# First down-projection weights split ahead of the last up chunk's convolution, kept sums added to the residual while weights stream, six pairs in the closing products

## The chip, the cores and the metric

The kernel runs on one core of one Trainium2 chip. The metric is the device time of one execution, in microseconds (us); lower is better. The time before is 957.09 us, the median of three runs between 956.24 and 958.12. Engines are named as in the profile: PE (matrix products), DVE (vector), ACT (scalar), POOL (GpSimd), SP (issues most transfers), and PSUM is the memory of eight banks into which PE sums.

## What is computed

A one-layer encoder trunk on 512 tokens of width 1024. The change lies in its last part, the gated MLP with a causal convolution, and in the residual and layer norm behind it:

```
z = h @ w_up                                  # 512 x 1024 by 1024 x 5632
zc = conv_b + sum_k conv_w[k] * shifted(z)    # three taps along the sequence
val, gate = split(zc)                         # 2816 each
y = (silu(gate) * val) @ w_down               # 2816 x 1024
x = layer_norm(ALPHA * x + gt_f * y) * ln_f_g + ln_f_b
```

Each product of 32-bit numbers is made from halves: an operand is cast to a short "hi" part (on ACT), the rest is its "lo" part (a subtraction on DVE), and three products hi·hi, hi·lo, lo·hi are summed.

## The kernel before, in words

**Up-projection.** The 44 column chunks of `w_up`, m = 0 to 43, are taken two by two, a value chunk and a gate chunk. Each takes 24 matmuls (`pzu`, L115, L116, L118). Its convolution follows: ACT takes the first tap out of PSUM (`zc`, L1521), DVE adds the other two (L1524, L1528). Then ACT does the silu (L1542), POOL multiplies gate and value (L1543). Two such products make one of eleven "pairs", p = 0 to 10, whose combinations are split into hi and lo: `xa` comes from the first product alone, `yh`, `xs`, `xh`, `ys` and their lo parts (L1458 to L1482) wait for the second one.

**Down-projection.** It is a product of 2 x 2 blocks done with seven products instead of eight (m1 to m7). The first sweep runs over the pairs and sums m1, m5, m6, m7, for two row tiles each, in all eight PSUM banks (`pd`). A step of it (`sweep_step`, L1583 on) is 24 matmuls and needs the pair's weights, which come by SP (`db0`, `db1`, `da`), are cast on ACT (`dbh`, `dah`) and subtracted on DVE (`dbl`, `dal`; L1559, L1560). Behind steps, `ahead` fetches and splits what the second sweep will need: the weights of pairs that are kept (`dr`, split into `d2..`, `d3..`, `d4..`, L1576, L1577) and, by POOL's transfers, left operands that had been written out (`z`, L1614). Step p = 10 ends the sums; `evacuate` takes them out of PSUM as `u1`, `u4`, `u3` and `c22` (L1667 to L1677).

The second sweep sums m2, m3, m4 (`pe`): for six pairs the weights (`dc`, `dd`) are streamed and split the same way, 18 matmuls a pair; for the R2 = 5 kept pairs the products are left to the end, where `close` makes them row tile by row tile. For each tile and half `final` then adds `u` to the bank (DVE, L1728), multiplies by the gate row `gt_f` (POOL, in the last row DVE, L1729), adds it to ALPHA·x (`residual`, DVE, L1688) and takes statistics (L1693); `row_end` (L1736 to L1757) does the layer norm and sends a row of tiles out. Three halves need no product of the second sweep's end and are done earlier, while pairs stream: `whole_half` for the two `c22` (POOL L1696, DVE L1688) and one `u3` (POOL L1723).

A scheduler sorts the instructions of each engine by the dependences and by priorities; each engine then does its list in order, and PE, ACT, DVE, POOL and SP wait for each other by semaphores. SP issues its transfers in its own list's order, so an issue that waits holds those behind it.

Of the kernel before, what the change touches and what calls it, by code (L numbers as in the profile page):

```python
# [15 lines left out]
P = 128  # L16
# [35 lines left out]
def trunk(ctx: ExitStack, tc: tile.TileContext, A, out):  # L52
# [22 lines left out]
    def pt_t(name, dt=F32):  # L75
        return sb.tile([P, 512], dt, name=name, tag="pt", bufs=8)
# [4 lines left out]
    def f(ap):  # L81
        return ap.bitcast(F32)
# [29 lines left out]
    def mm_chunk(o, wh, wl, xh, xl):  # L112
        cs = [slice(k * P, (k + 1) * P) for k in range(KT)]
        for k, c in enumerate(cs):
            nc.tensor.matmul(o, wh[:, c], xl[k], start=k == 0, stop=False)  # L115
            nc.tensor.matmul(o, wh[:, c], xh[k], start=False, stop=False)  # L116
        for k, c in enumerate(cs):
            nc.tensor.matmul(o, wl[:, c], xh[k], start=False, stop=k == KT - 1)  # L118
# [1372 lines left out]
    def ada_wide_piece(idx, k):  # L1491
# [3 lines left out]
        for n in range(2):  # L1495
# [4 lines left out]
            else:  # L1500
# [2 lines left out]
                    op0=ALU.mult, op1=ALU.add,  # L1503
                )

    held = [None]
    for i in range(NP):
        half = []
        for v in range(2):
            m = 2 * i + v  # L1510
            if m < NE:
                if v == 0:
                    up_early((m, m + 1), 1)
                pz = pzs[m]
# [6 lines left out]
            nc.scalar.activation(  # L1521
                t, pz, AF.Identity, bias=cols[:, cc + 3 : cc + 4], scale=cols[:, cc + 2 : cc + 3]
            )
            nc.vector.scalar_tensor_tensor(  # L1524
                out=t[:, 1:512], in0=pz[:, 0:511], scalar=cols[:, cc + 1 : cc + 2],
                in1=t[:, 1:512], op0=ALU.mult, op1=ALU.add,
            )
# [12 lines left out]
        if i == 5 + KT + 1:  # L1540
            gate_rows(3, "gtf")
        nc.scalar.activation(gate, gate, AF.Silu)  # L1542
        nc.gpsimd.tensor_tensor(out=val, in0=val, in1=gate, op=ALU.mult)  # L1543
# [8 lines left out]
    R2 = 5
    lo_half, hi_half = slice(0, 512), slice(512, 1024)

    def split_wide(parts, n, name):
        hi = wp.tile([P, D], F32R, name=name + "h", tag="whi")
        lo = wp.tile([P, D], F32R, name=name + "l", tag="wlo")
        for raw, c in parts:
            nc.scalar.copy(out=hi[:, c], in_=raw)  # L1559
            nc.vector.tensor_tensor(out=lo[:, c], in0=raw, in1=f(hi[:, c]), op=ALU.subtract)  # L1560
        return hi, lo

    def whole(src, name):
        raw = wp.tile([P, D], F32, name=name, tag="raw", bufs=3)
        nc.sync.dma_start(out=raw, in_=src)
        return raw

    def block(src, name, alloc=pad_t):
        raw = alloc(name)
        nc.sync.dma_start(out=raw[:, :512], in_=src)  # L1570
        return raw[:, :512]

    def split_block(raw, name, alloc):
        hi = alloc(name + "h")
        lo = alloc(name + "l")
        nc.scalar.copy(out=hi, in_=raw)  # L1576
        nc.vector.tensor_tensor(out=lo, in0=raw, in1=f(hi), op=ALU.subtract)  # L1577
        return hi, lo

    def wdn_row(k, c):  # L1580
        return A["wdn"][k * P : (k + 1) * P, c]
# [29 lines left out]
    def reload(p):  # L1611
        left2[p] = [act_t(f"z{i}{p}") for i in range(3)]
        for dst, src in zip(left2[p], spill[p]):
            nc.gpsimd.dma_start(out=dst, in_=src)  # L1614

    ws2 = {}

    def second_weights(p, alloc):
        srcs = ((2, wdn_row(2 * p + 1, lo_half)), (3, wdn_row(2 * p + 1, hi_half)), (4, t4_t[p]))
        raws = [(c, block(src, f"dr{c}", pt_t)) for c, src in srcs]  # L1620
        ws2[p] = {c: split_block(raw, f"d{c}{p}", alloc) for c, raw in raws}

    ahead = [(second_weights, HP - R2, h_t)]
    for i in range(R2 - 1):
        ahead += [(second_weights, HP - R2 + 1 + i, act_t), (reload, i)]
    ahead.append((reload, R2 - 1))
    free = 1 + 6
    for p in range(HP - 1):
        rb = [block(wdn_row(2 * p, lo_half), "db0"), block(t3_t[p], "db1")]
        ra = whole(wide_t[p], "da")  # L1630
        wb_ = split_wide(zip(rb, (lo_half, hi_half)), D, "db")
        wa_ = split_wide(((ra, slice(0, D)),), D, "da")
        x = lefts1(p)
        sweep_step(p, (
            (wb_, ((m1, x[1], lo_half), (m7, x[7], hi_half))),
            (wa_, ((m6, x[6], lo_half), (m5, x[5], hi_half))),
        ))
        while ahead and free >= (need := 6 if ahead[0][0] is second_weights else 3):
            work, *args = ahead.pop(0)
            work(*args)  # L1640
            free -= need
        free += 4
    p = HP - 1
    rb = [block(wdn_row(2 * p, lo_half), "db0"), block(t3_t[p], "db1")]
# [47 lines left out]
    def statistics(t, slot, n, c=slice(0, 512)):  # L1692
        return nc.vector.bn_stats(out=stats[t][:, slot, :], in_=x1[t][n][:, c])  # L1693

    def whole_half(t):
        nc.gpsimd.tensor_tensor(out=c22[t], in0=c22[t], in1=gt_f[1], op=ALU.mult)  # L1696
        residual(2 + t, 1, c22[t])
        if t == 0:
            statistics(2, 0, 1)
        else:  # L1700
            for i in range(2):
                statistics(3, i, 1, slice(i * 256, (i + 1) * 256))

    m2, m3, m4 = ([ps(f"pe{c}") for _ in range(2)] for c in (2, 3, 4))
    for p in range(HP - R2):
        rc = whole(A["wdn"][(2 * p + 1) * P : (2 * p + 2) * P, :], "dc")
        rd = block(t4_t[p], "dd")
        wc_ = split_wide(((rc, slice(0, D)),), D, "dc")
        wd_ = split_wide(((rd, lo_half),), 512, "dd")
        x = lefts2(p)  # L1710
        sweep_step(p, (
            (wc_, ((m2, x[2], lo_half), (m3, x[3], hi_half))),
            (wd_, ((m4, x[4], lo_half),)),
        ))
        if R2 + p < SPILLED:
            reload(R2 + p)
        if p < 2:
            whole_half(p)
        if p == 2:
            lnfg = row_tiles(4, h_t, "lnfg")  # L1720
            lnfb = row_tiles(5, h_t, "lnfb")
            q = pt_t("fq")
            nc.gpsimd.tensor_tensor(out=q, in0=u3[1], in1=gt_f[0], op=ALU.mult)  # L1723
            residual(3, 0, q)

    def final(t, n, acc, u, op, slot, eng):
        q = pt_t("fq")
        nc.vector.tensor_tensor(out=q, in0=u, in1=acc, op=op)  # L1728
        eng.tensor_tensor(out=q, in0=q, in1=gt_f[n], op=ALU.mult)  # L1729
        residual(t, n, q)  # L1730
        statistics(t, slot, n)

    def row_end(t, count):
# [168 lines left out]
```

## Time and profile before

| what | us |
|---|---|
| median of three runs | 957.09 (956.24 to 958.12) |
| the profiled execution, whole | 957.47 |
| its span in the profile | 955.7 |
| PE busy | 926.9 (97% of the span) |
| DVE busy | 676.0 (71%) |
| ACT busy | 408.6 (43%) |
| POOL busy | 279.2 (29%) |

The whole time holds 1.8 us that lie outside the span. A row of the timeline is: start, duration, engine, line, operation, the tile written and what it is made from, shapes, and in brackets how long the engine had stood idle before it and who released it. A row with "x2" stands for two in a row. A row of windows gives, for a stretch of time, each engine's busy us with its count of instructions, the clock granted to PE (1.00 is full), the busy share of the transfer engines and their GB/s. Lines are those of the kernel before.

### The profile page before, as it was taken

The page shows a single profiled execution, that of the slowest core. Times are in us where ns is not written, and L with a number is a line of the kernel's source. Part 1 is how long each engine was busy: PE and PEld are TensorE (multiplying, and loading weights), DVE is VectorE, ACT ScalarE, POOL GpSimd, SP SyncE. Part 2 cuts the span into 40 slices and gives each one's busy share as a digit, 9 for nine tenths or more (in the row PEclk, how much of TensorE's full clock was granted, in tenths as well). Part 3 has the DMA queues.
Part 4 walks back from the last instruction along what each step waited for, and adds up shares of the span by engine and source line. Part 5 has one row for each costly group of instructions (what it writes and reads, how often), then busy time and mean ns, then how long its engine had stood idle before and what let it go on. Part 6 is the DMA issues. An engine that isn't in the chain of part 4 may idle for free.

```text
span 955.7 us, 12643 instructions
## 1 busy us (share of the span) xinstructions
PE 926.9 (97%) x4453; PEld 780.4 (82%) x4453; DVE 676.0 (71%) x1043; ACT 408.6 (43%) x689; POOL 279.2 (29%) x339
## 2 busy tenths in 40 slices
PE   7999999999999999999999999999999999799993
PEld 6988888888888888888888889988888888588783
DVE  6967668546677798776475688688887566656848
ACT  4576555543324322233323435654444555456311
POOL 3741221122341154402153712122123211111514
PEclk9999999999999999999999999999999999799997
DMA  8913112134447986774575451155554534398902
GB/s 300 344 56 116 49 44 83 38 136 151 138 144 267 344 340 231 248 235 146 163 277 187 154 155 44 46 192 172 175 178 130 159 121 141 121 331 289 371 35 88
DMA packets 68159, 165.78 MB, mean 173 GB/s; under 512 B 9216, under 2 KB 12736, under 8 KB 68096
## 3 DMA queue, kind: packets, MB, share of 16 engines
q1 hardware_dynamic: 56880, 137.54, 42.7%
q0 software_dynamic: 10784, 26.89, 8.0%
q8 instruction: 35, 0.57, 0.2%
q10 hardware_dynamic: 432, 0.55, 0.2%
q14 instruction: 28, 0.23, 0.1%
HBM read 144.16 MB, written 20.78 MB: 173 GB/s over the span
## 4 chain that ended last, share of the span: by engine, by line
PE 82%; DVE 7%; DMA 6%; POOL 2%; issue 1%; ACT 1%; SPq 0%; DVEq 0%; POOLq 0%; ACTq 0%
PE pzu L116 7%; PE pzu L118 7%; PE pzu L115 7%; PE pg L115 4%; PE pg L116 4%; PE pg L118 4%; PE py L118 4%; PE py L115 4%; PE py L116 4%; PE pd L1590 2%; PE pd L1592 2%; PE pd L1593 2%; DMA ada<-in_ada1p 2%; PE pa L115 2%; PE pu L115 2%; PE pu L116 2%
## 5 line engine op out<-in xcount | busy, mean ns | idle before, releaser
L95 DVE TENSOR_TENSOR wupl<-wup,wuph 128x1024 fp32r<-128x1024 f32 x38 | 52.4, 1379 | 24.2 <-PE pzu L118 15.9
L1543 POOL TENSOR_TENSOR zc<-zc 128x512 f32<-128x512 f32 x22 | 29.8, 1354 | 131.4 <-ACT zc L1542 107.5
L94 ACT CAST wuph<-wup 128x1024 fp32r<-128x1024 f32 x38 | 40.1, 1054 | 46.4 <-PE pzu L116 33.9
L94 ACT CAST wbh<-wb 128x1024 fp32r<-128x1024 f32 x24 | 25.3, 1054 | 71.5 <-PE py L116 52.8
L985 POOL DMA_DIRECT2D wt<-wb x44 | 24.5, 556 | 77.1 <-DVE wb L981 72.0
L1521 ACT ACTIVATE zc<-pzu,cols 128x512 f32<-128x512 f32 x44 | 34.0, 777 | 24.9 <-PE pzu L118 20.5
L95 DVE TENSOR_TENSOR wgl<-wg,wgh 128x1024 fp32r<-128x1024 f32 x22 | 29.9, 1358 | 20.8 <-PE pg L118 10.1
L981 DVE TENSOR_TENSOR wb<-wb,wb 128x512 f32<-128x512 f32 x44 | 35.3, 806 | 6.2 <-DMA wb<-in_wdn 5.7
L1524 DVE SCALAR_TENSOR_TENSOR zc<-pzu,cols,zc 128x511 f32<-128x511 f32 x44 | 32.5, 743 | 9.3 <-ACT zc L1521 9.1
L856 DVE SCALAR_TENSOR_TENSOR ada<-adar,cact,ada 128x512 f32<-128x512 f32 x42 | 38.7, 961 | 0.4 <-DMA adar<-in_ada 0.4
L95 DVE TENSOR_TENSOR wbl<-wb,wbh 128x1024 fp32r<-128x1024 f32 x24 | 31.0, 1292 | 10.7 <-PE pg L118 5.4
L94 ACT CAST wgh<-wg 128x1024 fp32r<-128x1024 f32 x22 | 23.3, 1059 | 32.7 <-PE pg L116 20.3
L775 POOL TENSOR_SCALAR pe<-pe,mx 128x128 f32<-128x128 f32 (+3 forms) x32 | 17.0, 534 | 69.3 <-DVE mx L774 52.4
L1528 DVE SCALAR_TENSOR_TENSOR zc<-pzu,cols,zc 128x510 f32<-128x510 f32 x44 | 32.6, 744 | 0.7
L419 POOL TENSOR_TENSOR mg<-mg,th 128x512 f32<-128x512 f32 x16 | 28.5, 1779 | 12.7 <-DVE th L416 12.5
L1614 POOL DMA_DIRECT2D z<-ys x27 | 14.6, 542 | 56.7 <-PE pd L1590 35.0
L937 POOL TENSOR_TENSOR asum<-apad 128x527 f32<-128x527 f32 x8 | 12.3, 1544 | 54.6 <-ACT apad L932 28.0
L298 DVE SCALAR_TENSOR_TENSOR acc<-ada,cact,acc 128x256 f32<-128x256 f32 (+1 forms) x29 | 27.4, 944 | 1.0
L1542 ACT ACTIVATE zc<-zc 128x512 f32<-128x512 f32 x22 | 13.9, 631 | 23.7 <-DVE zc L1528 23.7
L1160 POOL TENSOR_TENSOR oraw<-oraw,gtt 128x512 f32<-128x512 f32 x6 | 9.8, 1645 | 42.0 <-DMA oraw<-in_wo 42.0
L1182 POOL TENSOR_TENSOR o<-o,gtt 128x512 f32<-128x512 f32 x10 | 17.5, 1772 | 12.2 <-DMA o<-in_wo 12.2
L771 ACT ACTIVATE pe<-sc,mx 128x128 f32<-128x128 f32 (+3 forms) x32 | 16.8, 528 | 8.8 <-DVE mx L769 7.5
(1541 smaller groups left out, 3239.1 us busy)
## 6 DMA issues: line engine op xcount, KB each, us to landing
wup<-in_wup SPq DMA_DIRECT2D x44, 512.0 KB, 3.6
wb<-in_wb SPq DMA_DIRECT2D x24, 512.0 KB, 3.8
adar<-in_ada SPq DMA_DIRECT2D x48, 256.0 KB, 4.8
wg<-in_wg SPq DMA_DIRECT2D x22, 512.0 KB, 3.6
wb<-in_wdn SPq DMA_DIRECT2D x44, 256.0 KB, 4.8
wt<-wb POOLq DMA_DIRECT2D x44, 256.0 KB, 4.0
z<-ys POOLq DMA_DIRECT2D x27, 256.0 KB, 6.8
ada<-in_ada1p SPq DMA_DIRECT2D x24, 256.0 KB, 5.0
```

What stands on the lines that cost most here:

```text
L94: nc.scalar.copy(out=hi[:, :n], in_=raw[:, :n])
L95: ins = nc.vector.tensor_tensor(out=lo[:, :n], in0=raw[:, :n], in1=f(hi[:, :n]), op=ALU.subtract)
L115: nc.tensor.matmul(o, wh[:, c], xl[k], start=k == 0, stop=False)
L116: nc.tensor.matmul(o, wh[:, c], xh[k], start=False, stop=False)
L118: nc.tensor.matmul(o, wl[:, c], xh[k], start=False, stop=k == KT - 1)
L419: nc.gpsimd.tensor_tensor(out=merged[m], in0=merged[m], in1=th, op=ALU.add)
L856: nc.vector.scalar_tensor_tensor(out=acc[n], in0=src, scalar=cact[:, k : k + 1], in1=acc[n], op0=ALU.mult, op1=ALU.add,)
L981: ins = nc.vector.tensor_tensor(out=dst, in0=x, in1=y, op=op)
L1521: nc.scalar.activation(t, pz, AF.Identity, bias=cols[:, cc + 3 : cc + 4], scale=cols[:, cc + 2 : cc + 3])
L1524: nc.vector.scalar_tensor_tensor(out=t[:, 1:512], in0=pz[:, 0:511], scalar=cols[:, cc + 1 : cc + 2], in1=t[:, 1:512], op0=ALU.mult, op1=AL ...
L1528: nc.vector.scalar_tensor_tensor(out=t[:, 2:512], in0=pz[:, 0:510], scalar=cols[:, cc : cc + 1], in1=t[:, 2:512], op0=ALU.mult, op1=ALU.add,)
L1543: nc.gpsimd.tensor_tensor(out=val, in0=val, in1=gate, op=ALU.mult)
```

## The change

It does four things. One: `first_weights(0)` is called after the matmuls of the last up chunk (m = 43) and before its convolution, so that the splits of pair 0's weights stand ahead of that convolution on ACT and DVE; for this the helpers move up in the file. Two: `ahead` takes nothing behind step 0 and at most two items behind each later step. Three: R2 goes from 5 to 6: five pairs stream, six are in the closes (in the order 6, 7, 9, 10, 8, 5), and pair 5's second weights (`d25`, `d35`, `d45`) are fetched at the end of the streamed pairs. Four: `fold` multiplies all eight evacuated sums by the gate row on POOL and adds them to the residual on DVE during streamed pairs 0 to 3, instead of three; `final` then multiplies the bank by the gate on DVE and adds it, with no POOL operation and no `u`.

```diff
+    R2 = 6
...
+    def first_weights(p):
+        rb = [block(wdn_row(2 * p, lo_half), "db0"), block(t3_t[p], "db1")]
+        ra = whole(wide_t[p], "da")
+        wb_ = split_wide(zip(rb, (lo_half, hi_half)), D, "db")
+        wa_ = split_wide(((ra, slice(0, D)),), D, "da")
+        return wb_, wa_
...
                 mm_chunk(pz, uh, ul, h2_hi, h2_lo)
+            if m == 2 * NP - 1:
+                opening = first_weights(0)
             cc = C_CONV + 4 * m
...
-        while ahead and free >= (need := 6 if ahead[0][0] is second_weights else 3):
-            work, *args = ahead.pop(0)
-            work(*args)
-            free -= need
+        for _ in range(2 if p else 0):
+            need = 6 if ahead and ahead[0][0] is second_weights else 3
+            if ahead and free >= need:
+                work, *args = ahead.pop(0)
+                work(*args)
+                free -= need
...
+    def fold(t, n, u):
+        nc.gpsimd.tensor_tensor(out=u, in0=u, in1=gt_f[n], op=ALU.mult)
+        residual(t, n, u)
...
-        if p < 2:
-            whole_half(p)
+        if p == 0:
+            fold_whole(0)
+            fold_whole(1)
+        if p == 1:
+            fold(0, 0, u1[0])
+            fold(1, 0, u1[1])
         if p == 2:
+            fold(0, 1, u4[0])
+            fold(1, 1, u4[1])
...
+        if p == 3:
+            fold(2, 0, u3[0])
+            fold(3, 0, u3[1])
+    second_weights(HP - R2, h_t, pad_t)
+    closing = [HP - 5, HP - 4, HP - 2, HP - 1, HP - 3, HP - 6]
...
-    def final(t, n, acc, u, op, slot, eng):
+    def final(t, n, acc, op, slot):
         q = pt_t("fq")
-        nc.vector.tensor_tensor(out=q, in0=u, in1=acc, op=op)
-        eng.tensor_tensor(out=q, in0=q, in1=gt_f[n], op=ALU.mult)
-        residual(t, n, q)
+        nc.vector.tensor_tensor(out=q, in0=acc, in1=gt_f[n], op=ALU.mult)
+        nc.vector.tensor_tensor(out=x1[t][n], in0=x1[t][n], in1=q, op=op)
         statistics(t, slot, n)
```

Three places show what the lists of the engines make of it. The first is DVE where the up-projection ends; `zc` rows are the convolutions of the last two chunks, and `db`/`da` the weights of pair 0 (before: db_7689 and db_7691; after: db_7655 and db_7657) and pair 1 (after: db_7729). Before:

```order
L1524 SCALAR_TENSOR_TENSOR zc<-pzu,cols,zc 128x511
L1528 SCALAR_TENSOR_TENSOR zc<-pzu,cols,zc 128x510
L1475 TENSOR_TENSOR se<-zc 128x256
L1475 TENSOR_TENSOR sd<-zc 128x256
L1475 TENSOR_TENSOR sd<-se,zc 128x256
L1482 TENSOR_TENSOR yl_7671<-zc,yh_7670 128x512
L1459 TENSOR_TENSOR xs_7667<-se,xs_7667 128x256
L1475 TENSOR_TENSOR se<-zc,sd 128x256
L1480 TENSOR_TENSOR xl_7669<-sd,xh_7668 128x512
L1560 TENSOR_TENSOR dbl<-db_7689,dbh 128x512
L1560 TENSOR_TENSOR dal<-da,dah 128x1024
L1459 TENSOR_TENSOR ys_7672<-se,ys_7672 128x256
```

And after:

```order
L1514 TENSOR_TENSOR dbl<-db_7655,dbh 128x512
L1514 TENSOR_TENSOR dbl<-db_7657,dbh 128x512
L1459 TENSOR_TENSOR xa_7586<-zc,xa_7586 128x256
L1564 SCALAR_TENSOR_TENSOR zc<-pzu,cols,zc 128x511
L1568 SCALAR_TENSOR_TENSOR zc<-pzu,cols,zc 128x510
L1514 TENSOR_TENSOR dal<-da,dah 128x1024
L1564 SCALAR_TENSOR_TENSOR zc<-pzu,cols,zc 128x511
L1568 SCALAR_TENSOR_TENSOR zc<-pzu,cols,zc 128x510
```

Pair 0's subtractions moved ahead of the last convolutions, `dal` directly in front of the last one; where they stood, pair 1's now stand (from db_7729 on). On ACT the casts moved in the same way. The second place is SP's list there; `wt_2216` to `wt_2219` are the `da` weights of pairs 0 to 3, `dr` the weights kept for the second sweep. Before:

```order
L1565 DMA da<-wt_2216 128x1024
L1565 DMA da<-wt_2217 128x1024
L1565 DMA da<-wt_2218 128x1024
L1570 DMA db_7689<-in_wdn 128x512
L1570 DMA db_7691<-wt_2227 128x512
L1570 DMA db_7747<-in_wdn 128x512
L1570 DMA dr_7729<-in_wdn 128x512
```

And after:

```order
L1519 DMA da<-wt_2216 128x1024
L1524 DMA db_7655<-in_wdn 128x512
L1524 DMA db_7657<-wt_2227 128x512
L1519 DMA da<-wt_2217 128x1024
L1519 DMA da<-wt_2218 128x1024
L1519 DMA da<-wt_2219 128x1024
L1524 DMA db_7729<-in_wdn 128x512
L1524 DMA db_7731<-wt_2228 128x512
L1524 DMA db_7787<-in_wdn 128x512
L1524 DMA dr_7769<-in_wdn 128x512
```

Pair 0's `db` moved to the front, and pair 3's `da`, which goes into one of three buffers and so needs pair 0's to be free, now stands ahead of pair 1's two `db`. The third place is POOL behind the first sweep; `z` are the reloads of the second sweep's left operands, `gtf` the gate row. Before:

```order
L1614 DMA z_8353<-ys_5772 128x512
L1614 DMA z_8354<-ys_5773 128x512
L1723 TENSOR_TENSOR fq<-u_8263,gtf_7073 128x512
L1696 TENSOR_TENSOR c_8268<-c_8268,gtf_7075 128x512
L1696 TENSOR_TENSOR c_8274<-c_8274,gtf_7075 128x512
L1614 DMA z_8392<-ys_5774 128x512
```

And after:

```order
L1704 TENSOR_TENSOR u_8238<-u_8238,gtf_7073 128x512
L1704 TENSOR_TENSOR u_8243<-u_8243,gtf_7073 128x512
L1623 DMA z_8356<-ys_5771 128x512
L1623 DMA z_8357<-ys_5772 128x512
L1623 DMA z_8358<-ys_5773 128x512
L1704 TENSOR_TENSOR c_8268<-c_8268,gtf_7075 128x512
L1704 TENSOR_TENSOR u_8258<-u_8258,gtf_7073 128x512
L1704 TENSOR_TENSOR u_8248<-u_8248,gtf_7075 128x512
L1704 TENSOR_TENSOR c_8274<-c_8274,gtf_7075 128x512
L1704 TENSOR_TENSOR u_8263<-u_8263,gtf_7073 128x512
L1704 TENSOR_TENSOR u_8253<-u_8253,gtf_7075 128x512
L1623 DMA z_8396<-ys_5774 128x512
```

Three multiplies became eight, six of them in a row ahead of the last six reloads. DVE's list has the eight residual adds (L1696 of the kernel after) between the splits of the streamed weights: two are ahead of the second streamed pair's `dcl`, the others follow one by one up to the fourth pair's.

More of the change, by code (lines that the diff above doesn't have):

```diff
@@ L1504, in ada_wide_piece, with split_wide, whole, block @@
                 )
+    R2 = 6
+    lo_half, hi_half = slice(0, 512), slice(512, 1024)
+    def split_wide(parts, n, name):
+        hi = wp.tile([P, D], F32R, name=name + "h", tag="whi")
+        lo = wp.tile([P, D], F32R, name=name + "l", tag="wlo")
+        for raw, c in parts:
+            nc.scalar.copy(out=hi[:, c], in_=raw)
+            nc.vector.tensor_tensor(out=lo[:, c], in0=raw, in1=f(hi[:, c]), op=ALU.subtract)
+        return hi, lo
+    def whole(src, name):
+        raw = wp.tile([P, D], F32, name=name, tag="raw", bufs=3)
+        nc.sync.dma_start(out=raw, in_=src)
+        return raw
+    def block(src, name, alloc=pad_t):
+        raw = alloc(name)
+        nc.sync.dma_start(out=raw[:, :512], in_=src)
+        return raw[:, :512]
+    def split_block(raw, name, alloc):
+        hi = alloc(name + "h")
+        lo = alloc(name + "l")
+        nc.scalar.copy(out=hi, in_=raw)
+        nc.vector.tensor_tensor(out=lo, in0=raw, in1=f(hi), op=ALU.subtract)
+        return hi, lo
+    def wdn_row(k, c):
+        return A["wdn"][k * P : (k + 1) * P, c]
+    def first_weights(p):
[4 more added lines that the diff above has]
+        return wb_, wa_
     held = [None]
@@ L1551, in trunk @@
     gt_f = [gate_row[3, n] for n in range(2)]
[L1552 to L1581, printed above, removed]
     def sweep_step(p, chunks):
@@ L1616, in trunk, with second_weights @@
     ws2 = {}
-    def second_weights(p, alloc):
+    def second_weights(p, alloc, raw_alloc=pt_t):
         srcs = ((2, wdn_row(2 * p + 1, lo_half)), (3, wdn_row(2 * p + 1, hi_half)), (4, t4_t[p]))
-        raws = [(c, block(src, f"dr{c}", pt_t)) for c, src in srcs]
+        raws = [(c, block(src, f"dr{c}", raw_alloc)) for c, src in srcs]
         ws2[p] = {c: split_block(raw, f"d{c}{p}", alloc) for c, raw in raws}
[L1623 to L1626, printed above, removed]
+    ahead = [(second_weights, HP - R2 + 1, h_t)]
+    for i in range(R2 - 2):
+        ahead += [(second_weights, HP - R2 + 2 + i, act_t), (reload, i)]
+    ahead.append((reload, R2 - 2))
     free = 1 + 6
     for p in range(HP - 1):
[L1629 to L1632, printed above, removed]
+        wb_, wa_ = first_weights(p) if p else opening
         x = lefts1(p)
@@ L1693, in statistics, with fold_whole @@
         return nc.vector.bn_stats(out=stats[t][:, slot, :], in_=x1[t][n][:, c])
-    def whole_half(t):
-        nc.gpsimd.tensor_tensor(out=c22[t], in0=c22[t], in1=gt_f[1], op=ALU.mult)
-        residual(2 + t, 1, c22[t])
+    def fold(t, n, u):
+        nc.gpsimd.tensor_tensor(out=u, in0=u, in1=gt_f[n], op=ALU.mult)
+        residual(t, n, u)
+    def fold_whole(t):
+        fold(2 + t, 1, c22[t])
         if t == 0:
@@ L1714, in trunk @@
         ))
-        if R2 + p < SPILLED:
-            reload(R2 + p)
-        if p < 2:
-            whole_half(p)
+        if R2 - 1 + p < SPILLED:
+            reload(R2 - 1 + p)
+        if p == 0:
[4 more added lines that the diff above has]
+            fold(1, 0, u1[1])
         if p == 2:
+            fold(0, 1, u4[0])
+            fold(1, 1, u4[1])
             lnfg = row_tiles(4, h_t, "lnfg")
             lnfb = row_tiles(5, h_t, "lnfb")
-            q = pt_t("fq")
-            nc.gpsimd.tensor_tensor(out=q, in0=u3[1], in1=gt_f[0], op=ALU.mult)
-            residual(3, 0, q)
-    def final(t, n, acc, u, op, slot, eng):
+        if p == 3:
[4 more added lines that the diff above has]
+    def final(t, n, acc, op, slot):
         q = pt_t("fq")
-        nc.vector.tensor_tensor(out=q, in0=u, in1=acc, op=op)
-        eng.tensor_tensor(out=q, in0=q, in1=gt_f[n], op=ALU.mult)
-        residual(t, n, q)
+        nc.vector.tensor_tensor(out=q, in0=acc, in1=gt_f[n], op=ALU.mult)
+        nc.vector.tensor_tensor(out=x1[t][n], in0=x1[t][n], in1=q, op=op)
         statistics(t, slot, n)
@@ L1764, in products @@
         def products():
-            for p in range(HP - R2, HP):
+            for p in closing:
                 xh, xl = lefts2(p)[c]
@@ L1769, in products @@
                     acc, xh[:, ts_], xl[:, ts_], wh[:, cols_], wl[:, cols_],
-                    start and p == HP - R2, p == HP - 1,
+                    start and p == closing[0], p == closing[-1],
                 )
@@ L1777, in trunk @@
     for t in range(2):
-        eng = (nc.gpsimd, nc.vector)[t]
         close(2, m2[t], t)
-        final(t, 0, m2[t], u1[t], ALU.add, 0, nc.gpsimd)
+        final(t, 0, m2[t], ALU.add, 0)
         close(3, m3[t], t)
-        final(t, 1, m3[t], u4[t], ALU.add, 1, eng)
+        final(t, 1, m3[t], ALU.add, 1)
         row_end(t, 2)
@@ L1785, in trunk @@
             close(4, m4[0], 0)
-            final(2, 0, m4[0], u3[0], ALU.subtract, 1, nc.gpsimd)
+            final(2, 0, m4[0], ALU.subtract, 1)
             row_end(2, 2)
```

## The prediction

> **What bounds the kernel now.** I read the page first: its head, the engines' busy times and the chain that ended last.
>
> ```profile
> span 955.7 us, 12643 instructions
> PE 926.9 (97%) x4453; PEld 780.4 (82%) x4453; DVE 676.0 (71%) x1043; ACT 408.6 (43%) x689; POOL 279.2 (29%) x339
> PE 82%; DVE 7%; DMA 6%; POOL 2%; issue 1%; ACT 1%; SPq 0%; DVEq 0%; POOLq 0%; ACTq 0%
> ```
>
> PE is the bound. So time can come from three places only: where PE stands idle, where it runs at a low clock, and what lies behind its last matmul. I looked for the first two with the windows around the end of the up-projection and through both sweeps.
>
> ```profile
> core 0: us, PE busy (x) PEld busy (x) DVE busy (x) ACT busy (x) POOL busy (x), PEclk, DMA share, GB/s
> 824.50:826.60 2.10, 0.00 (x0) 0.00 (x0) 1.22 (x2) 0.78 (x1) 0.00 (x0) 1.00 0.00 0
> 826.60:831.30 4.70, 0.00 (x0) 0.00 (x0) 2.54 (x7) 2.69 (x6) 1.26 (x1) 0.50 0.15 56
> 831.30:836.80 5.50, 5.36 (x12) 3.69 (x13) 5.19 (x9) 4.14 (x9) 0.00 (x0) 0.50 0.84 257
> 840.00:860.00 20.00, 20.00 (x90) 16.57 (x89) 12.96 (x18) 11.13 (x18) 3.03 (x6) 1.00 0.99 334
> 880.00:902.00 22.00, 21.86 (x97) 17.80 (x96) 18.19 (x23) 8.71 (x13) 12.35 (x19) 1.00 1.03 346
> ```
>
> PE is idle from 824.5 to 831.3, and the granted clock falls to half at 826.6 and returns at 836.8. After that PE is full; in the second sweep's first third (880 to 902) it loses 0.14 us. The timeline of the hole says what ends it:
>
> ```profile
> 824.11 0.39 PE L118 MATMUL pzu<-h2T7h,wupl 128*128 128x512 f32 x1
> 824.53 0.78 ACT L1521 ACTIVATE zc<-pzu,cols 128x512 f32<-128x512 f32 x1 [4.66 <-PE pzu L118]
> 825.34 0.75 DVE L1524 SCALAR_TENSOR_TENSOR zc<-pzu,cols,zc 128x511 f32<-128x511 f32 x1 [3.90 <-ACT zc L1521]
> 827.74 1.26 POOL L1543 TENSOR_TENSOR zc<-zc 128x512 f32<-128x512 f32 x1 [9.27 <-ACT zc L1542]
> 829.03 1.46 SPq L1570 DMA_DIRECT2D dr<-in_wdn  x2
> 829.04 0.62 ACT L1481 CAST yh<-zc 128x512 fp32r<-128x512 f32 x1 [1.44 <-POOL zc L1543]
> 830.17 0.62 ACT L1479 CAST xh<-sd 128x512 fp32r<-128x512 f32 x1 [0.20 <-DVE sd L1475]
> 830.69 0.61 ACT L1559 CAST dbh<-db 128x512 fp32r<-128x512 f32 x1
> 831.36 0.80 PE L1592 MATMUL pd<-dbh,xa 128*128 128x512 f32 x1 [6.86 <-ACT dbh L1559]
> 831.92 0.68 DVE L1560 TENSOR_TENSOR dbl<-db,dbh 128x512 fp32r<-128x512 f32 x1
> 832.53 1.22 DVE L1560 TENSOR_TENSOR dal<-da,dah 128x1024 fp32r<-128x1024 f32 x1
> 839.75 0.39 PE L1592 MATMUL pd<-dbh,xa 128*128 128x512 f32 x1
> 847.20 1.14 ACT L1559 CAST dbh<-db 128x512 fp32r<-128x512 f32 x2 [2.33 <-PE pd L1593]
> ```
>
> The last matmul of the up-projection starts at 824.11. Pair 0's first matmul starts at 831.36, released by the cast `dbh`, which stands on ACT behind the whole chain convolution, silu, POOL, `yh`, `xs`, `xh`. Its left operand `xa` belongs to the earlier half of a pair and the bracket names no transfer, so what holds it is the cast's place in ACT's list. At half clock step 0 takes until 839.75, 8.39 us; a step at full clock is 24 matmuls by 20.00/90 = 0.222 to the 0.227 between starts (the windows lose a record or two), 5.44 us. The hole and the slow step cost 7.0 + 2.95 = 9.95 us.
>
> Last I read DVE, POOL and PE in two places, the second sweep's start and the end; these are the rows that matter of each.
>
> ```profile
> 889.19 1.23 DVE L1560 TENSOR_TENSOR dcl<-dc,dch 128x1024 fp32r<-128x1024 f32 x1 [2.45 <-ACT ddh L1559]
> 891.02 1.37 DVE L1670 TENSOR_TENSOR u<-pd,u 128x512 f32<-128x512 f32 x2
> 893.02 2.65 POOL L1614 DMA_DIRECT2D z<-ys  x5 [2.87 <-PE pd L110]
> 894.15 0.39 PE L1592 MATMUL pe<-dch,z 128*128 128x512 f32 x1
> 896.95 2.55 POOL L1696 TENSOR_TENSOR c<-c,gtf 128x512 f32<-128x512 f32 x2
> 897.03 3.02 DVE L1688 SCALAR_TENSOR_TENSOR x<-x,fq 128x512 f32<-128x512 f32 x1 [0.88 <-POOL fq L1723]
> ```
>
> ```profile
> 922.97 0.69 DVE L1728 TENSOR_TENSOR fq<-u,pe 128x512 f32<-128x512 f32 x1 [6.05 <-PE pe L110]
> 928.59 0.69 DVE L1688 SCALAR_TENSOR_TENSOR x<-x,fq 128x512 f32<-128x512 f32 x1 [1.46 <-POOL fq L1729]
> 935.70 17.26 SPq L1757 DMA_DIRECT2D out<-x  x8
> 939.03 1.28 POOL L1751 TENSOR_TENSOR x<-x,lnfb 128x512 f32<-128x512 f32 x1 [1.15 <-ACT x L1750]
> 939.25 1.61 DVE L1753 SCALAR_TENSOR_TENSOR x<-x,rs,lnfb 128x512 f32<-128x512 f32 x1
> 939.84 0.28 PE L110 MATMUL pe4x<-d410h,yh 128*128 128x256 f32 x1
> 941.39 0.67 DVE L1793 TENSOR_TENSOR fq<-pe,gtf 128x512 f32<-128x512 f32 x1
> 941.98 0.68 DVE L1729 TENSOR_TENSOR fq<-fq,gtf 128x512 f32<-128x512 f32 x1
> 944.11 0.41 DVE L1693 BATCH_NORM_STATS2 std<-x 128x6 f32<-128x256 f32 x1
> 945.70 0.38 DVE L1736 BATCH_NORM_AGGREGATE mv<-std 128x2 f32<-128x12 f32 x2
> 946.00 1.41 DVE L1741 SCALAR_TENSOR_TENSOR x<-x,mv,lnfg 128x512 f32<-128x512 f32 x2
> 948.71 3.28 DVE L1753 SCALAR_TENSOR_TENSOR x<-x,rs,lnfb 128x512 f32<-128x512 f32 x3
> ```
>
> Two things are to be seen. A DVE operation with two inputs from SBUF stretches while POOL multiplies: the residual add at 897.03 took 3.02 us, as long as POOL's two multiplies (896.95 to 899.50), against 0.68 for a like operation alone at 941.98; at 939.25 one took 1.61 beside a POOL operation of 1.28. And DVE, not PE, sets the end: PE is done at 940.12, DVE at 951.99, 11.87 us later; the last output is issued by 952.96.
>
> **The seam.** After the change pair 0's casts (two of about 0.57, one of about 1.0) lie in ACT's idle 4.66 us and its `dbl` in DVE's idle 3.90 us before the last convolution, both shown in brackets above; they cost nothing there. `dal` stands directly ahead of the last chunk's additions on DVE. It can start when PE frees the buffer of the last up weights, at about 824.5, and runs 1.14; the convolution, which started at 825.34, starts 0.34 later. That is a late start for everything down to `xh` of about 0.2 to 0.35. Step 0 now fills the hole, 824.34 to 829.78 at full clock. Next in ACT's list, in the place where pair 0's `dbh` stood, is pair 1's: 830.69 + 0.2, so step 1 starts at about 831.55, after a gap of 1.8 us; it then waits for its `dbl`, which DVE gives behind `xl`, for 0.4, as PE stood 0.5 after four matmuls in step 0. At full clock step 1 ends at 831.55 + 5.44 + 0.4 = 837.4, against 839.75 + 5.44 = 845.2 before. Gain: **7.8 us**. The bounds: 9.95 if the gap were nothing, and 5.0 if step 1 runs at half clock like step 0 does today.
>
> **SP.** Pair 3's `da` needs pair 0's raw buffer, freed by `dal` at 825.8, and pair 1's `db` stand behind it. They are issued at about 826.3; pair 1's cast comes 4.4 us later, so they are in time. The first `dr` issues keep their place behind the last conv tiles. But the run of transfers that starts at 829.03 today starts only 3 us earlier, while PE asks 7.8 us earlier, and between 840 and 860 the transfer engines are 0.99 busy: no spare. The lead is what pays: at 847.20 the cast of `db` had waited 2.33 us for PE, not for a transfer. So steps 2 to 4 come late by 7.8 − 3 − 2.3 = 2.5 at most; by nothing if the three `dr` a step, which now come a step later, make up for it. I take the middle, **+1.2**. The splits that `ahead` does move a step later; their number is the same, and DVE and ACT are busy 13 and 11 of 20 us there: nothing.
>
> **The second sweep's start.** The 1.2 shifts all engines alike and is left out here. DVE begins the evacuations at 883.3 (from 891.02). Until the second streamed pair's `ddl` is done it has eight evacuations and two residual adds by 0.60 to 0.68 (the start-to-start of 941.39 and 941.98, and half of the row at 891.02), 6.4 in all, `dcl` 1.14 (the 1.23 at 889.19, less the overlap), `d25l` 0.60 and `ddl` 0.68: 8.8 us, until 892.1. POOL runs eight multiplies of 1.28 in the same 14 us, six in a row, and `dcl`, `d25l`, `ddl` and one add are operations with two SBUF inputs. If the engines alternate, as at 939.25, each waits up to one multiply: about 0.3 + 0.9 + 1.25 + 1.25 = 3.7, so `ddl` ends at 895.8 to 896.2. PE enters the sweep at 894.15 − 7.8 = 886.35 and needs it 16 matmuls into the second pair: 886.35 + 4.08 + 3.63 = 894.05. Gap: 2.1, at a `ddl` of 896.1. Then two adds, each one multiply late (2 × 1.85), statistics 0.6 and the third pair's `dcl` 1.22 end 5.5 us later, at 901.6; PE, released at 896.1, needs it after 2 more matmuls and 12 of the next pair, 3.2 us later: a gap of 2.3. The multiplies are then over. Sum 4.4, less the 0.14 of today: **+4.2**. Ends: 0, if DVE were not held (8.8 us then suffice), and 6.5 if DVE's second add and the splits get in only when the six multiplies (7.7 us) are over, as at 897.03. I take alternation because the single-operation row is the nearer case: POOL's list has other work after the first two, and DVE's list differs at each step. The last six `z` reloads wait behind the six multiplies, from 893 to 902 instead of 899.4; their data is for the closes, ten us later. Cover: those ten us.
>
> [...]
>
> **PE's own work.** One pair moves from the stream (18 matmuls) to the closes: the same columns, three halves more instructions of half width. 0. The new order of the closes and pair 5's splits (three casts, three subtractions, in DVE's list behind the third pair's) lie beside 20 us of streaming: 0.
>
> **The end.** The finals lose the addition of `u`, POOL's multiply of 1.28 and its two handovers (1.46 us of DVE's idleness at 928.59). PE's last two closes are 36 half-width matmuls, 4.2 us. Meanwhile DVE does, for the third row tile's last half and the first half of the fourth: five operations of 0.60, small ones 0.35 (945.70), two of L1741 1.41 (946.00), statistics 0.35 (944.11): 5.1. So at PE's end it is 0.9 behind. Then: gate multiply 0.35, the third row's last step 0.66, held for POOL's 1.28 before the 0.40 add, statistics 0.41, aggregate and add 0.38, 1.41, 0.74, 0.41: 6.0. DVE ends 6.9 us after PE instead of 11.87. **−5.0**; ends 0 and −6.3 (no hold).
>
> **Sum.** −7.8 + 1.2 + 4.2 − 5.0 = −7.4. The profiled execution took 957.47, 0.38 above the median of the runs shown; 957.47 − 7.4 = **950.1 us**. That 0.38 is within what is left open; 0.2% (1.9 us) is about what a measurement of this kernel can tell from no change.
>
> **Rivals.** First, *the clock falls in a new gap*. Today it fell 2.1 us after the last matmul ended (824.50 to 826.60) and stayed low through 5.5 us of work, which cost 2.95. The change makes three gaps of about 2 us (before step 1, and two in the second sweep). Each is just at that length. A fall costs between 0 and 2.95, and DVE catches up meanwhile; one fall, 1.9: 952.0; two: 953.9. For it: the row at 826.60. Against: there PE was idle before and after; the new gaps are enclosed by full work. [...]
>
> Second, *the folds cost nothing*: DVE is held by POOL only where the two start together, and 8.8 us suffice; 950.1 − 4.2 = 945.9. The rows at 897.03 and 939.25 speak against it.
>
> Third, *the end stays DVE's*: the late DVE of the second sweep carries its lag into the closes, and the finals start as late as today relative to PE: the 5.0 don't come, 955.1. Against it: DVE waited 6.05 us for PE before its first final, at 922.97.
>
> Fourth, *the seam's gain is smaller*: the change does not do what it says at step 1, as step 1's operands wait for the same chain and run at half clock: 5.0 instead of 7.8, with the rest 952.9.
>
> Fifth, the other side, *slower*: the clock falls at the first gap of the second sweep and is kept low because each streamed pair again ends in a gap. Four pairs of 4.08 us at half clock add 16.3; less the 4.2 of gaps that PE's slowness then hides, 950.1 + 12.1 = 962. Against it: at half clock a pair gives DVE 8.2 us, more than it needs, so gaps end and the clock returns after some 5.5 us of work, as at 836.8. It decides from the third slow pair on.
>
> **How the numbers follow.** Forecast 0.55, its own range 948.8 to 951.5 (the transfers' 0 to 2.5). Clock falls 0.22; folds free 0.06; end unchanged 0.06; seam smaller 0.06; slower 0.05. The range, 947.9 to 953.3, leaves out the slower case, the third, the second and two falls of the clock (0.03), 0.20 in all. Faster by over 0.2% are all but the fifth and the third joined with a fall of the clock: 0.93; within 0.2%: 0.03; slower: 0.04.
>
> **What would show it.** PE's matmuls of step 0 directly behind the last `pzu`, at full clock; one gap of under 2 us before step 1, released by ACT's `dbh`; DVE's L1696 and L1514 of 1.8 us or more beside POOL's L1704, and two PE gaps of about 2 us released by DVE's `ddl` and `dcl`; DVE's end 7 us behind PE's. Wrong would make it: PEclk under 1.00 in the 20 us from the first pair on, PE waits released by ACT casts that themselves wait for transfers between 840 and 855, or finals that start behind a late DVE.

## The result and the profile after

The changed kernel takes 953.45 us (median of six runs, 952.53 to 954.29), against 957.48 us for the kernel before, timed beside it (median of six): ratio 0.9953, 95% interval 0.9935 to 0.9971. It is faster by 4.0 us; 7.0 below the median of 957.09 were forecast, with a range of 3.8 to 9.2. So the gain lies at the low edge of the range; 953.45 as it stands is 0.15 us above the range's upper end, 953.3, because the kernel before was 0.4 slower this time. The profiled execution took 952.53.

The head of its page, then the windows through the second sweep's start (columns as before):

```profile
span 950.8 us, 12652 instructions
PE 925.1 (97%) x4456; PEld 779.7 (82%) x4456; DVE 683.8 (72%) x1048; ACT 409.0 (43%) x690; POOL 282.1 (30%) x340
```

```profile
889.00:895.40 6.40, 6.40 (x30) 5.10 (x28) 5.91 (x5) 2.20 (x3) 6.38 (x8) 1.00 1.12 393
895.40:897.00 1.60, 0.18 (x1) 0.00 (x0) 1.60 (x1) 0.00 (x0) 1.60 (x2) 1.00 1.02 325
897.00:901.70 4.70, 0.00 (x0) 0.00 (x0) 4.70 (x3) 0.00 (x0) 4.70 (x6) 0.58 0.03 9
901.70:904.30 2.60, 2.55 (x6) 2.07 (x7) 2.60 (x5) 1.67 (x2) 1.24 (x3) 0.50 0.96 296
```

PE, full before, now stands idle here for six us and then works at half clock for nearly three more (until 904.6). The timeline of the seam and of the first steps:

```profile
822.95 0.39 PE L118 MATMUL pzu<-h2T7h,wupl 128*128 128x512 f32 x1
823.18 0.39 PE L1601 MATMUL pd<-dbh,xa 128*128 128x512 f32 x1
829.95 0.61 ACT L1513 CAST dbh<-db 128x512 fp32r<-128x512 f32 x1
830.61 0.50 PE L1601 MATMUL pd<-dbh,xa 128*128 128x512 f32 x1 [1.83 <-ACT dbh L1513]
836.58 0.39 PE L1601 MATMUL pd<-dbh,xa 128*128 128x512 f32 x1
841.12 0.62 ACT L1530 CAST d27h<-dr 128x512 fp32r<-128x512 f32 x1 [4.42 <-DMA dr<-in_wdn]
842.56 0.62 ACT L1530 CAST d37h<-dr 128x512 fp32r<-128x512 f32 x1 [0.83 <-DMA dr<-in_wdn]
843.60 0.62 ACT L1530 CAST d47h<-dr 128x512 fp32r<-128x512 f32 x1 [0.42 <-DMA dr<-wt]
844.12 1.13 ACT L1513 CAST dbh<-db 128x512 fp32r<-128x512 f32 x2
844.79 0.50 PE L1601 MATMUL pd<-dbh,xa 128*128 128x512 f32 x1 [2.61 <-ACT dbh L1513]
```

Step 0 now follows the last `pzu` matmul at once (823.18). Steps 1 and 2 start at 830.61 and 836.58. Step 3, due 5.44 later, starts at 844.79: its `dbh` stands on ACT behind three casts for kept pairs, each of which waits for its own transfer `dr`.

The second sweep's start, DVE, POOL and PE:

```profile
889.91 2.75 DVE L1696 SCALAR_TENSOR_TENSOR x<-x,u 128x512 f32<-128x512 f32 x1 [0.49 <-POOL u L1704]
893.79 5.71 DVE L1696 SCALAR_TENSOR_TENSOR x<-x,u 128x512 f32<-128x512 f32 x1
899.42 2.28 DVE L1514 TENSOR_TENSOR dcl<-dc,dch 128x1024 fp32r<-128x1024 f32 x1
892.74 1.31 POOL L1704 TENSOR_TENSOR c<-c,gtf 128x512 f32<-128x512 f32 x1
894.00 2.51 POOL L1704 TENSOR_TENSOR u<-u,gtf 128x512 f32<-128x512 f32 x2
896.47 1.25 POOL L1704 TENSOR_TENSOR c<-c,gtf 128x512 f32<-128x512 f32 x1
897.68 2.92 POOL L1704 TENSOR_TENSOR u<-u,gtf 128x512 f32<-128x512 f32 x2
901.75 1.22 PE L1599 MATMUL pe<-dcl,z 128*128 128x512 f32 x2 [6.17 <-DVE dcl L1514]
```

One residual add of 0.68 us of work, which starts at 893.79 while POOL's first multiply of the row runs, is done only at 899.50, after five of the six; the `dcl` behind it waits for the sixth. PE waits 6.17 us for that `dcl`. And the end:

```profile
941.42 0.28 PE L110 MATMUL pe4x<-d45h,z 128*128 128x256 f32 x1
946.29 1.14 DVE L1771 SCALAR_TENSOR_TENSOR x<-x,rs,lnfb 128x512 f32<-128x512 f32 x2
943.28 1.88 POOL L1769 TENSOR_TENSOR x<-x,lnfb 128x512 f32<-128x512 f32 x1 [1.15 <-ACT x L1768]
```

DVE is done at 947.43, 5.73 us after PE's 941.70.

### The profile page after: what moved, and what is told of

Read it like the earlier page. It is cut to its first block, busy times and chain, and to the rows that moved or that the text cites. A ratio compares the mean times of both kernels' runs of the same rounds, so it can differ in the third digit from the quotient of the medians.

```text
span 950.8 us, 12652 instructions
## 1 busy us (share of the span) xinstructions
PE 925.1 (97%) x4456; PEld 779.7 (82%) x4456; DVE 683.8 (72%) x1048; ACT 409.0 (43%) x690; POOL 282.1 (30%) x340
```

## The experiments

Times are medians; the ratio is to the kernel before, timed beside each. In the code, "..." marks what is left out. "Step 1" is the second pair of the first sweep.

**The two halves of the change apart (e1, e2).** e1 is the kernel before, with these lines of the change alone (the helpers moved up, R2 = 5, old finals and folds):

```diff
+            if m == 2 * NP - 1:
+                opening = first_weights(0)
...
-        while ahead and free >= (need := 6 if ahead[0][0] is second_weights else 3):
+        for _ in range(2 if p else 0):
```

> The kernel before with only the first two parts of the change (pair 0's first weights split ahead of the last convolution; at most two items of the work ahead per step, from step 1). My theory: the seam gives PE 7.45 us and the wait before step 3 takes 2.6 back, the rest is as before: about 4.7 us below the kernel before, 952.6. Rival (PE's earlier arrival is eaten in the second sweep whatever the folds do): 1 us or less below it. The profile should show one PE wait of about 1.8 us before step 1, one of about 2.5 before step 3, and none over 0.5 in the second sweep.

Measured: 951.48 us, ratio 0.9934 (0.9918 to 0.995). The seam is worth 6.3 us, more than the whole change and more than the 4.7 expected; the prediction's first two terms come to 6.6. The waits of PE from the seam on, and the end:

```profile
PE pd L1601 <- ACT dbh L1512: 2.1, 2, 1.8
933.44 0.28 PE L110 MATMUL pe4x<-d410h,yh 128*128 128x256 f32 x1
942.30 3.28 DVE L1761 SCALAR_TENSOR_TENSOR x<-x,rs,lnfb 128x512 f32<-128x512 f32 x3
```

The second sweep has no wait, as expected; DVE ends 11.86 us behind PE, as in the kernel before. The expected wait before step 3 was not in this profile (the second wait of the line, 0.3, stands before step 4): here the clock fell after the 1.8 us gap, step 1 took 7.20 us instead of 5.97, and the `dr` were in time for the later PE.

e2 is the other half: the changed kernel with the lines above undone.

> The changed kernel with its first two parts undone: the seam and the work ahead are as before, six pairs in the closes, eight folds, finals without POOL. My theory: the row of multiplies on POOL costs PE 6 us and the clock about 1.4 more, the end gives 6.1 back: between 0 and 2.5 us slower than the kernel before, about 958.5. Rival (the gap comes only because PE arrives earlier than the transfers and DVE are ready): no gap over 1 us and about 5 us faster, 952.

Measured: 958.63 us, ratio 1.0012 (1.0002 to 1.0023), as expected.

```profile
PE pe L1597 <- DVE dcl L1514: 6.2, 1, 6.2
```

The gap is there, as long, though PE comes 5 us later to the sweep (893.69, against 888.62 in the changed kernel). The rival falls: it is not PE's earlier arrival that makes it. What the shorter end gives, this gap takes. Alone the halves give −6.3 and +0.8, together −4.0; where the other 1.5 us come from was not tested. The wait before step 3, which e1's profile has not, may be part of it.

**Where the 6.2 us come from (e3, e5, e6, e7, e8).** e3 holds each fold's multiply on POOL behind the reloads of its pair:

```diff
+            last_reload[:] = [nc.gpsimd.dma_start(out=dst, in_=src).ins]
...
-        nc.gpsimd.tensor_tensor(out=u, in0=u, in1=gt_f[n], op=ALU.mult)
+        with tc.issue_after(last_reload[0]):
+            nc.gpsimd.tensor_tensor(out=u, in0=u, in1=gt_f[n], op=ALU.mult)
```

> The changed kernel, with each fold's multiply put on POOL behind the last reload of its streamed pair, so that the eight multiplies come in groups of four, two and two, the later two groups waiting for PE as the reloads do. The work is the same. My theory (DVE's operation with two SBUF inputs is kept out until POOL's row of multiplies is over): the gap of 6.1 us falls to 1 to 3 and the clock does not fall: 4 to 6 us below the changed kernel, about 948.5. Rival (the DVE queue is too long, whatever POOL does, since it has eight adds to do): the gap stays over 4 and the time within 2 us of the changed kernel.

Measured: 952.64 us, ratio 0.9948 (0.9929 to 0.9966): 0.8 below the changed kernel, not the 4 to 6 of my theory. DVE and POOL:

```profile
892.04 5.15 DVE L1698 SCALAR_TENSOR_TENSOR x<-x,u 128x512 f32<-128x512 f32 x1 [0.88 <-POOL u L1707]
897.12 2.63 DVE L1514 TENSOR_TENSOR dcl<-dc,dch 128x1024 fp32r<-128x1024 f32 x1
894.46 1.28 POOL L1707 TENSOR_TENSOR c<-c,gtf 128x512 f32<-128x512 f32 x1
897.38 3.50 POOL L1707 TENSOR_TENSOR u<-u,gtf 128x512 f32<-128x512 f32 x2
```

In the group of four one add, freed by the first multiply, was held through the other three and beyond (the fourth ends at 895.74, the add at 897.19). In the next group of two the `dcl` ran after the first and the second multiply waited for it: they alternated. PE's wait was 3.7 us, and the clock fell. This left both readings open, so the next run takes the multiplies out. From here on the kernels start from e4 (below). e5 leaves the eight multiplies by the gate row out:

```diff
     def fold(t, n, u):
-        nc.gpsimd.tensor_tensor(out=u, in0=u, in1=gt_f[n], op=ALU.mult)
         residual(t, n, u)
```

> The kernel of e4 (the changed kernel with pair 3's casts ahead on ACT), leaving out the eight multiplies of the evacuated sums by the gate row, so that its output is not the reference's; DVE keeps all eight adds. My theory (DVE is kept out by POOL): the 6.1 us gap falls below 0.7 and the clock stays full, 7 us below e4, about 943.5. Rival (DVE's own queue is too long by the eight adds): a gap of 3 us or more is left, and the time is 947 or more.

Measured: 943.11 us, ratio 0.9848 (0.9832 to 0.9865), 7.7 below e4. All that is left of the gap, with the eight adds still in DVE's list:

```profile
PE pe L1601 <- DVE dcl L1516: 0.4, 1, 0.4
```

So the queue is not too long by the adds. POOL still issues its reloads there, and these alone hold nothing: an add beside them takes 0.68 us.

```profile
891.30 0.68 DVE L1699 SCALAR_TENSOR_TENSOR x<-x,u 128x512 f32<-128x512 f32 x1
891.38 1.07 POOL L1625 DMA_DIRECT2D z<-ys  x2 [0.59 <-PE pe L1601]
```

e6 gives the multiplies to DVE:

```diff
-        nc.gpsimd.tensor_tensor(out=u, in0=u, in1=gt_f[n], op=ALU.mult)
+        nc.vector.tensor_tensor(out=u, in0=u, in1=gt_f[n], op=ALU.mult)
```

> The kernel of e4 with the eight multiplies done by DVE instead of POOL. My theory: DVE's queue until the second pair's ddl is then 8 evacuations, 8 multiplies, 2 adds and the splits, 13.5 us, none of them held, so PE waits about 2 us for ddl and under 1 for the next dcl, without a fall of the clock: 4 to 5 us below e4, about 946. Rival (POOL's multiplies cost DVE no more than their own time): the 4.8 us that DVE gets more make the gap longer than e4's 6.1, and the time is 951 or more.

Measured: 946.67 us, ratio 0.9886 (0.9872 to 0.9901), 4.1 below e4, though DVE has 4.8 us more to do (eight operations of 0.60). PE's waits, in the second sweep now both for `dcl`:

```profile
PE pe L1601 <- DVE dcl L1516: 1.9, 2, 1.6
PE pd L1603 <- ACT dbh L1515: 1.8, 1, 1.8
```

So what cost PE its time is not the amount of the folds' arithmetic but that POOL, while it does it, shuts DVE out, as the rows of the changed kernel show (the add of 893.79 took 5.71 us, against 0.68 alone). e7 fixes POOL's list to three reloads, two multiplies, and so on:

```diff
+            if last_pool:
+                order.enter_context(tc.issue_after(last_pool[0]))
...
+        with tc.issue_after(last_pool[0]):
+            last_pool[:] = [nc.gpsimd.tensor_tensor(out=u, in0=u, in1=gt_f[n], op=ALU.mult).ins]
...
```

> The kernel of e4 with POOL's list fixed to three reloads, two multiplies, three reloads, two multiplies and so on, u1 first, so that never more than two multiplies stand together. My theory (a waiting operation of DVE gets in when the row of multiplies is over, so the cost goes with the length of the row): no DVE operation takes over 3.2 us, PE's gap is 1 to 3 us and the clock stays full: 4 to 6 us below e4, about 945.5. Rival (each DVE operation waits about as long whatever the row, because the reloads' issue on POOL holds it too): a DVE add of 4 us or more and a gap over 4.

Measured: 950.66 us, ratio 0.993 (0.9915 to 0.9945), 0.1 below e4: my theory's number fails. Its rows:

```profile
891.42 2.88 DVE L1705 SCALAR_TENSOR_TENSOR x<-x,u 128x512 f32<-128x512 f32 x1
894.23 2.72 DVE L1516 TENSOR_TENSOR dcl<-dc,dch 128x1024 fp32r<-128x1024 f32 x1
901.62 3.35 DVE L1516 TENSOR_TENSOR dcl<-dc,dch 128x1024 fp32r<-128x1024 f32 x1
890.39 2.55 POOL L1714 TENSOR_TENSOR c<-c,gtf 128x512 f32<-128x512 f32 x2
892.89 1.67 POOL L1630 DMA_DIRECT2D z<-ys  x3
```

No single operation waits as long as before (2.7 to 3.4 instead of 5.7), but more of them wait, and the add of 891.42 ends 1.36 us after the second multiply (892.94), with POOL already issuing reloads; PE's waits sum to 3.8 + 1.1 and the clock fell again. Neither forecast holds: with shorter rows the longest single wait is shorter, but the loss as a whole stays the same.

e8 tests the form of the operation: ACT multiplies x by ALPHA during the first sweep, one tile a step, and DVE's fold is a plain addition.

```diff
+                    nc.scalar.mul(x1[(p - 1) // 2][(p - 1) % 2], x1[(p - 1) // 2][(p - 1) % 2], ALPHA)
...
-        residual(t, n, u)
+        nc.vector.tensor_tensor(out=x1[t][n], in0=x1[t][n], in1=u, op=ALU.add)
```

> The kernel of e4 with ACT multiplying x by ALPHA during the first sweep (one tile a step), so that DVE's fold is a plain two-input addition (TENSOR_TENSOR) in the place of the scaled one (SCALAR_TENSOR_TENSOR); POOL's list is that of e4, six multiplies in a row. If the form of the operation decides whether DVE gets in between two multiplies (the subtractions in e3 waited for one, the scaled adds for two to five): no DVE operation over 2.6 us, a gap of about 2, 945 to 947. If the length of POOL's row decides, as I hold more likely: the add of x_10 again takes over 4.5 us, the gap is about 6, and the time is within 1 us of e4.

Measured: 951.46 us, ratio 0.9941 (0.9926 to 0.9955), within 0.7 of e4.

```profile
892.92 6.74 DVE L1713 TENSOR_TENSOR x<-x,u 128x512 f32<-128x512 f32 x1
891.68 1.31 POOL L1712 TENSOR_TENSOR c<-c,gtf 128x512 f32<-128x512 f32 x1
896.64 2.47 POOL L1712 TENSOR_TENSOR u<-u,gtf 128x512 f32<-128x512 f32 x2
```

The plain addition waits until the row of six is over (899.11), even longer. The form is not what decides.

**The wait before step 3 (e4).** The kept pairs' casts go behind the cast of `da` of the same step, and none is taken at step 2:

```diff
+            last_cast[:] = [nc.scalar.copy(out=hi[:, c], in_=raw).ins]
...
-            if ahead and free >= need:
+            if p != 2 and ahead and free >= need:
                 work, *args = ahead.pop(0)
-                work(*args)
+                with tc.issue_after(last_cast[0]):
+                    work(*args)
```

> The changed kernel, with the casts for kept pairs on ACT put behind the cast of da of the same step, and none taken at step 2, so that pair 3's dbh stands ahead of d27h, d37h, d47h. My theory: PE's wait of 2.6 us before step 3 comes from dbh standing behind casts that wait for dr, and falls below 0.5: 2 to 2.5 us below the changed kernel, 951.2. Rival (the transfers of the first weights are late themselves, the engines being 1.0 busy): the wait stays or moves to step 4 or 5, and the time is within 0.7 us of the changed kernel.

Measured: 950.79 us, ratio 0.9926 (0.9911 to 0.9942), 2.7 below the changed kernel. PE's waits:

```profile
PE pe L1601 <- DVE dcl L1516: 6.2, 1, 6.2
PE pd L1603 <- ACT dbh L1515: 1.8, 1, 1.8
```

Only the gap before step 1 is left in the first sweep; the wait before step 3 is gone and came back at no later step. In this profile the clock fell at the seam, which alone would give the `dr` more time; but e6 and e7 have the same list, full clock there, and no such wait either. In e6 pair 3's cast waited for PE, not for its transfer:

```profile
838.94 1.16 ACT L1515 CAST dbh<-db 128x512 fp32r<-128x512 f32 x2 [1.85 <-PE pd L1604]
```

So it was the place in ACT's list, not late first weights.

**Two steps on (e9, e10).** e9 puts each fold of e6, both operations on DVE, behind the subtractions of its streamed pair:

```diff
+        with tc.issue_after(last_sub[0]):
+            nc.vector.tensor_tensor(out=u, in0=u, in1=gt_f[n], op=ALU.mult)
+            residual(t, n, u)
...
```

> The kernel of e6 with each fold (multiply and add, both on DVE) put in DVE's list behind the subtractions of its streamed pair, and u1 folded first, c22 second. My theory (PE's 1.6 us wait in e6 comes from four multiplies and four adds that stand ahead of the next pair's dcl): no wait over 0.7 us in the second sweep, 1 to 2 us below e6, about 945.2. Rival (DVE has too much to do in the streamed pairs wherever it stands): the same wait moves to a later pair and the time is within 0.5 us of e6.

Measured: 943.43 us, ratio 0.9857 (0.9843 to 0.987), 3.2 below e6, more than the 1 to 2 expected; no wait in the second sweep. In the profiles that sweep is 3.3 us shorter (48.66, then 45.39), of which e6's listed waits are 1.9; the rest is not explained. The whole list of PE's waits from the seam on is the gap before step 1:

```profile
PE pd L1604 <- ACT dbh L1516: 1.8, 1, 1.8
```

e10 fetches and splits pair 1's first weights ahead of the last silu too:

```diff
         nc.scalar.activation(gate, gate, AF.Silu)
+        if i == NP - 1:
+            second = first_weights(1)
...
```

> The kernel of e9 with pair 1's first weights also fetched and split ahead of the last silu and its lefts (which only step 10 needs). My theory (PE waits 1.8 us before step 1 only because dbh of pair 1 stands behind yh, xs and xh on ACT): that wait falls below 0.5 and the time by 1.3 to 1.8 us against e9, about 943.6. Rival (transfers: what PE gains before step 1 it waits for dbh at steps 2 to 5): within 0.5 us of e9.

Measured: 940.03 us, ratio 0.9826 (0.9813 to 0.984), 3.4 below e9 and the fastest version. The wait before step 1 is gone; one of 0.6 is left:

```profile
PE pd L1606 <- ACT dah L1516: 0.6, 1, 0.6
```

The gain is more than the 1.3 to 1.8 expected. In the profiles the way from the last `pzu` matmul to step 3 is 3.9 us shorter: 1.8 are the gap and 1.4 the clock, which in e9 had fallen behind the gap, so that step 1 took 7.36 us against 5.97 at full clock. The rival is true in part: in e10 step 5 waits for the `dah` of the line above, and step 6 starts 0.9 us late.

## Why the prediction was right or wrong, step by step

The profiled executions differ by 957.47 − 952.53 = 4.94 us. Of this 1.16 arose before the seam (the last `pzu` matmul at 824.11 and 822.95), where the lists are the same; I count it as difference between executions. The rest, by the prediction's steps:

| step | forecast | profile |
|---|---|---|
| seam (last `pzu` matmul to start of step 2: 21.08, then 13.63) | −7.8 | −7.45 |
| first sweep (start of step 2 to the second sweep: 48.96, then 52.04) | +1.2 | +3.1 |
| second sweep (its start to PE's end: 45.97, then 53.08) | +4.2 | +7.1 |
| DVE's end behind PE's (11.87, then 5.73) | −5.0 | −6.1 |
| behind DVE's end | 0 | −0.4 |
| sum | −7.4 | −3.8 |

**Right: the seam**, in size and course: step 0 in the hole, a gap of 1.83 released by `dbh` of pair 1 (1.8 forecast), then a short wait for `dbl`: step 1 took 5.97 (5.84 forecast). **Right: the end**, if larger than forecast; −6.1 lies near the bound "no hold", −6.3: where POOL and DVE met, at 943.28, it was POOL's sum that stretched, to 1.88, against 1.28 in the kernel before (939.03).

**Wrong: the transfers' +1.2**, both in size and in mechanism. The step that failed is the sentence that the splits which `ahead` moves cost nothing because DVE and ACT are half idle. I counted ACT's busy time and not its order: casts that wait for late `dr` stand in front of the cast PE waits for. First weights were not late; e4, e6 and e7 show that the wait goes with the order in that list. It makes step 3 2.8 us late, more than the stated bound of 2.5; the other 0.3 us are spread over the sweep. One of the prediction's own signs of being wrong came with it: a PE wait behind ACT casts that wait for transfers, between 840 and 855.

**Wrong: the second sweep's +4.2.** The step that failed is the choice between the two ends: alternation, after the single-operation row at 939.25, instead of the row at 897.03, where two multiplies in a row had held an add for both. The nearest row was the one with a row of multiplies, and with it the stated end of 6.5 met the 6.2 us of the gap. Another 1.4 us is the clock, which fell 2.2 us into the longer gap and stood at half until 904.6, so that six matmuls took 2.72 us instead of 1.36: the first rival's mechanism, riding on the second term's error. Gap and clock make 7.5, 0.4 more than the row's change.

**The total.** That the time came out at the edge of the range is partly luck. The two wrong terms cost 4.8 us more than forecast, and the end gave 1.1 more. 953.45 is near the 953.9 that the first rival had for two falls of the clock, but in this profile one fall cost 1.4 and the waits the rest.

**Rivals.** The folds for nothing, an unchanged end and the slower case did not come. The clock rival came twice: in the second sweep, and, in some executions, behind the seam's gap (below). The fourth rival's slow step 1 is not in this profile, but came in part with those falls: in e9 the gap of 1.84 us was followed by one, and step 1 took 7.36 us.

## What to carry to other kernels

A multiply "for nothing" on POOL was not free here, while DVE had operations with two SBUF inputs on PE's path: eight multiplies of 1.25 us cost 7.7 us on POOL (e5 against e4) and, in DVE's own list behind the subtractions, nothing that PE waited for (e9). When work is moved ahead, look at what stands in front of the operation PE waits for, on its engine, and at what that waits for; that an engine is half idle says nothing (ACT, 43% busy, made PE wait 2.6 us before step 3). A last chunk's chain that is needed only much later should stand behind the next stage's first operands (6.3 us in e1).

## What was not expected of the hardware

**DVE shut out.** An add waited 5.1 us on top of its own work, through five multiplies, and 6.1 in e8, through the row's end; in other places DVE and POOL alternated (e3's `dcl` at 897.12, of 2.63 us, waited for one multiply). So a whole row of POOL's operations went ahead of one waiting DVE operation. Not every DVE operation was held: the evacuation ahead of that add, which has one input in PSUM, took 0.68 us beside the row's first multiply (892.74 to 894.05):

```profile
893.19 0.68 DVE L1685 TENSOR_TENSOR u<-pd,u 128x512 f32<-128x512 f32 x1
```

What lets DVE in between was not settled: the form of the operation does not (6.74 us in e8), and in e3 and e7 an add also ended 1.45 and 1.36 us after a row, while POOL issued reloads, though beside such issues alone an add took 0.68 in e5.

**The clock at short gaps.** Nine of the profiled kernels have the same gap of 1.8 us before step 1. In the changed kernel, e3, e6 and e7 the clock stayed full and step 1 took 5.97 to 5.99 us; in e1, e4, e5, e8 and e9 it fell and step 1 took 7.20 to 7.58. The granted clock, as recorded, tells more. It stood at half for 3.41 us in e9 (831.17 to 834.59), for 6.83 in the changed kernel (897.79 to 904.62) and for 10.24 in the kernel before (826.59 to 836.83); then it stood at full for 40.96 in the changed kernel (until 945.58) and for 105.81 in the kernel before (until 942.64). These are 1, 2, 3, 12 and 31 times 3.413. Steps of this length, laid back from each kernel's own changes over the seam, sort the nine kernels. First the step of e9 that holds the whole gap (828.50 to 830.34), and the one behind it; then the two of e6, which cut the gap at 830.63:

```profile
827.76:831.17 3.41, 1.57 (x8) 0.95 (x6) 3.15 (x8) 2.95 (x6) 0.22 (x1) 1.00 0.85 302
831.17:834.59 3.42, 3.42 (x9) 2.37 (x8) 3.42 (x6) 2.46 (x6) 0.00 (x0) 0.50 0.88 245
```

```profile
827.22:830.63 3.41, 1.90 (x9) 1.24 (x7) 2.00 (x6) 1.79 (x4) 1.29 (x1) 1.00 0.95 356
830.63:834.04 3.41, 2.97 (x12) 2.16 (x13) 3.41 (x7) 3.09 (x6) 0.00 (x0) 1.00 0.84 263
```

In the five kernels whose clock fell, PE was idle for 1.71 to 1.86 us of one such step; in the four others for 1.52 at most. So in these nine the outcome went with where the same gap lay against the steps; in e9 the fall, at 831.17, came when PE had been at work again since 830.34. How much idleness it takes is not settled: of the other steps at full clock, those with 2.10 us idle (the kernel before, 823.18 to 826.59) or more were followed by a fall and those with 1.61 (the changed kernel, 843.18 to 846.59) or less were not, but some of 1.7 to 1.9 (in e3, e5, e6 and e7) were not either, and no run moved the gap against the steps by itself.
